# Eight chunks of the conditioning product moved from the value stage to the attention stage of a one-core encoder block

## The chip, the cores and the metric

The kernel runs on one core of a Trainium2 chip. The metric is device time in microseconds, median of three runs. The engines are named as the profile names them: PE (TensorE matmuls), PEld (its weight loads), DVE (VectorE), ACT (ScalarE), POOL (GpSimd) and SP (SyncE, whose queue issues nearly all DMAs here).

## The reference

One encoder block on x of 1024 positions by 1024 channels. Only the lines that touch the change:

```python
ada = jax.nn.silu(c) @ w_ada[i] + b_ada[i]          # (1, 6144)
shift1, scale1, gate1, shift2, scale2, gate2 = [t[:, None, :] for t in jnp.split(ada, 6, axis=-1)]
h = rmsnorm(x, g_mix[i]) * (1 + scale1) + shift1
proj = h @ w_in[i]                                   # q, k, v of two attentions, two gates
...
x = x + gate1 * (merged @ w_out[i])
h2 = rmsnorm(x, g_ffn[i]) * (1 + scale2) + shift2
...
x = x + gate2 * (glu @ w_down[i])
```

The first third of the product, shift1 and scale1 (2048 of 6144 columns), is needed at once. The other 4096 columns, gate1, shift2, scale2 and gate2, are first used after the attention: `ada[:, 24:32]` by `dshift` (L1001), `ada[:, 32:40]` by `am2` (L497), `ada[:, 16:24]` in `out_tile` (L1016), the rest in `acc` (L983) and at the end.

## The kernel before

**Planner.** All instructions are written in Python in program order. Outside blocks marked `manual_schedule` a planner orders them on each engine: at each moment of its own timeline an engine takes, of what is ready, the instruction that stands earliest in the program. A tile gets a buffer of its pool when its first writer is placed, so loads into one kind of buffer are served in program order. The order that results is fixed; on the chip each engine runs it in order.

**Product in halves.** Every projection is an fp32 product made of three fp32r matmuls: a weight tile of 128 columns is loaded as 512 KB into a `wraw` buffer (`w_load`, L58; there are two), split by ACT into `whi` (L55) and by POOL into `wlo` (L56; two of each), and `product` (L72) issues for each of eight k and each half of the positions `whi*hi`, `whi*lo`, `wlo*hi` (L77 to L79) into one of two PSUM banks `pj`. `q_half`, `k_half` and `gate_tile` empty the bank (ACT L392, L427, L732; DVE L393, L429). The `wraw` buffer is free once it is split.

**Conditioning product.** One chunk is 512 columns. `ada_load` (L126) loads its eight row tiles as four 512 KB transfers; DVE scales the first by silu(c) (L155) and adds the other seven to it (L157, 128x512 each, all in SBUF); `ada_sums` (L135) sums over partitions with four 128x1 matmuls against a column of ones (L141, in the profile eight of them, two passes each) into a PSUM tile `pada`; `ada_bias` adds the bias (L148). Chunks 0 to 3 feed norm1 in a prologue ordered by hand. Chunk 4 and 5 end that prologue (L351, L368, L369). Chunks 6 to 11 follow the value products in the loop at L485, two after each half of the value columns.

**Stages.** Prologue with norm1 (to about 100 us), the value products of both branches (L247 to L249, to about 182 us), the attention stage, the gate products that are left, then the merge, the FFN and the final norm. In the attention stage the program has for n = 0 to 7: `attend_dil` or `attend_na` of head pair n, then the q and k products of pair n+1 (`qk_tiles`), then `counts[n]` gate tiles (2, 2, 2, 2, 1, 1, 0); the last six gate tiles stand behind the loop. The q, k and gate products run while attention work waits; below they are called fillers. Attention itself uses PSUM tiles `S`, `T` and `O` (two each): scores (L557, L587, L683), a bias add and maximum on DVE (L541, L687), exponential on ACT, transposes into `T`, a split by ACT and DVE, and the product into `O`.

Of the kernel before, what the change touches and what calls it, by code (L numbers as in the profile page):

```python
# [9 lines left out]
FT = mybir.dt.float32  # L10
FR = mybir.dt.float32r
AF = mybir.ActivationFunctionType
OP = mybir.AluOpType
# [5 lines left out]
KT = 8  # L19
# [6 lines left out]
NA_NC = (6, 8, 8, 6)  # L26


def hybrid_encoder(tc, xT, c, w_ada, small, w_in, p1_bias, p23_bias, na_bias, ln2_mult, ident, w_br, w_out,
                   w_up, w_down, out):  # L30
    nc = tc.nc
    act, dve, pool, pe, sp = nc.scalar, nc.vector, nc.gpsimd, nc.tensor, nc.sync
# [83 lines left out]
    slots = iter(range(1 << 20))  # L116

    def wada_tile(j):
        n = next(slots) if j < 4 else -1
        if n == 0:  # L120
            return qkpool.tile([128, 2, 512], FT, name="kl")
        if n > 0 and (n - 1) % 6 < 2:
            return early.tile([128, 2, 512], FT, name="wada", bufs=2)
        return adapool.tile([128, 2, 512], FT, name="wada", bufs=4)

    def ada_load(j):  # L126

        rows = []
        for t in range(0, KT, 2):
            wt = wada_tile(j)  # L130
            sp.dma_start(wt, w_ada[j][:, t:t + 2])
            rows += [wt[:, i] for i in range(2)]
        return rows

    def ada_sums(parts, pa=None, stop=True, n=4):  # L135

        first = pa is None
        pa = ps_s.tile([128, 4], FT, name="pada", bufs=1) if first else pa
        for i, (w, col) in enumerate(parts):
            for m in range(n):  # L140
                pe.matmul(pa[:, m:m + 1], w[:, m * 128:(m + 1) * 128], col, start=first and i + m == 0,  # L141
                          stop=stop and i == len(parts) - 1 and m == n - 1, skip_group_check=True)
        return pa

    def ada_bias(c0, pa, n=4):

        cc = slice(c0, c0 + n)
        dve.tensor_tensor(ada[:, cc], pa[:, :n], b_ada[:, cc], OP.add)  # L148

    def ada_rows(wt, ts, acc=None):  # L150

        for t in ts:
            if acc is None:
                acc = wt[t]
                dve.tensor_scalar(acc, acc, cs[:, t:t + 1], None, OP.mult)  # L155
            else:
                dve.scalar_tensor_tensor(acc, wt[t], cs[:, t:t + 1], acc, OP.mult, OP.add)  # L157
# [6 lines left out]

    def ada_join(wt, a, b):
        dve.tensor_tensor(wt[a], wt[a], wt[b], OP.add)

    def ada_chunk(j, wt):
        ada_rows(wt, range(KT))
        ada_bias(4 * j, ada_sums([(wt[0], ones)]))  # L170

    def x_load(hf, ks=range(KT)):
        x = []
# [114 lines left out]
    with tc.manual_schedule(engines={e.engine for e in (sp, act, dve, pool, pe)}):  # L288
        x = [x_load(0)]
        sp.dma_start(sm, small)  # L290
        wt = {0: ada_load(0)}
        qk_raw = [wpool.tile([128, KT, 128], FT, name="wraw") for _ in range(2)]
        half_load(qk_raw, (0, 4), 0)
        v_raw = [qkpool.tile([128, KT, 128], FT, name="kl") for _ in range(2)]
        half_load(v_raw, (8, 9), 0)
        wt[1] = ada_load(1)
        wt[2] = ada_load(2)
        half_load(qk_raw, (0, 4), 1)
        half_load(v_raw, (8, 9), 1)
        wt[3] = ada_load(3)  # L300
        qk_w = [[wpool.tile([128, KT, 128], FR, name=n) for n in ("whi", "wlo")] for _ in range(2)]
        v_w = [v_tiles()]
        qk_psum = [ps_g.tile([128, 512], FT, name="pj") for _ in range(2)]

        accs = sq_accs()
        square(x[0], accs, range(8), dve)
        pcol = square_sums(accs)
        pb = norm_bcast(pcol)
        ada_rows_pool(wt[0], range(3))
        ada_rows(wt[0], range(3, 7))  # L310
        ada_join(wt[0], 3, 0)
        bc = to_sbuf(pb)
        pa = ada_sums([(wt[0][7], cs[:, 7:8]), (wt[0][3], ones)])
        scale_x(x[0], pb, None, range(2), dve)
        qk_split(0, (pool, dve))
        v_split(v_raw, (pool, dve), slice(0, 4), v_w[0])
        scale_x(x[0], pb, bc, range(2, 4), pool)
        piece_bias(0, pa)
        modulate(x[0], 0, range(2), (dve, dve))
        qk_products(range(2))  # L320
        pvs = [v_banks()]
        ada_rows_pool(wt[1], range(3))
        for q in range(1, 4):
            ks, c = range(2 * q - 2, 2 * q), 2 * q
            p = (0, 3, 4, 4)[q]
            ada_rows(wt[q], range(p, (8, 7)[q > 1]))
            ada_join(wt[q], p, 0)
            pa = ada_sums([(wt[q][7], cs[:, 7:8])], stop=False) if q > 1 else None
            v_products(0, (0, 1), ks)
            pa = ada_sums([(wt[q][p], ones)], pa)  # L330
            v_products(0, (2, 3), ks)
            if q == 1:
                scale_x(x[0], pb, bc, range(4, 6), pool)
            if q == 2:
                qk_split(1, (pool, dve))
                v_split(v_raw, (pool, dve), slice(4, 8), v_w[0])
                scale_x(x[0], pb, bc, range(6, 8), pool)
            if q < 3:
                ada_rows_pool(wt[q + 1], range(4))
            else:  # L340
                x.append(x_load(1, range(4)))
                v_raw1 = v_load(0, 1)
                x[1] += x_load(1, range(4, 8))
                accs = sq_accs()
                square(x[1], accs, range(3), dve)
            piece_bias(q, pa)
            modulate(x[0], 0, range(c, c + 2), (dve, dve))
            qk_products(range(c, c + 2))
        v_products(0, range(4), range(6, 8))
        v_w.append(v_split(v_raw1, (dve, pool)))  # L350
        ada_w = ada_load(4)  # L351
        square(x[1], accs, range(3, 8), dve)
        for st in range(4):
            v_out(0, 0, st, pvs[0][st])
        pvs.append(v_banks())
        v_products(1, (0,), range(8))
        pcol = square_sums(accs)
        v_products(1, (1,), range(8))
        pb = norm_bcast(pcol)
        v_products(1, (2, 3), range(8))  # L360
        bc = to_sbuf(pb)
        scale_x(x[1], pb, bc, range(0, 8, 2), dve)
        scale_x(x[1], pb, bc, range(1, 8, 2), pool)
        modulate(x[1], 1, range(4), (dve, pool))
        for st in range(4):
            v_out(0, 1, st, pvs[1][st])
        modulate(x[1], 1, range(4, 8), (dve, pool))
        ada_chunk(4, ada_w)  # L368
        ada_chunk(5, ada_load(5))  # L369

    def qk_tiles(br, pr, ws=None, ps=None):
        qt, kt = ((0, 4), (12, 16))[br]
# [112 lines left out]
    for br in range(2):  # L485
        for hv in range(2):
            w = v_split(v_load(br, hv), (pool, pool)) if br else v_w[hv]
            for st in range(8):
                if br or st > 3:
                    v_out(br, hv, st, v_product(st, w))  # L490
            if br == 0:
                va_chunks(slice(hv * 256, hv * 256 + 256))
            for j in range(2):
                jj = 6 + 4 * br + 2 * hv + j
                if jj < 12:
                    ada_chunk(jj, ada_load(jj))
    dve.scalar_tensor_tensor(am2, ada[:, 32:40], 1.0, g_ffn, OP.add, OP.mult)  # L497
    work.release()
    adapool.release()
    early.release()  # L500
# [225 lines left out]
    def gate_tile(t):  # L726
        w = weights(w_in[24 + t], pool)
        for hf, cols in enumerate(halves):
# [3 lines left out]
            act.activation(g, p, AF.Copy)  # L732
            sp.dma_start(g_scr[t][:, cols], g)

    gspool = tc.alloc_tile_pool(name="gs", bufs=2, side="right", reuse_waits="tile")
    with tc.tile_pool(name="at", bufs=2, reuse_waits="tile") as work:
        lnm = sm_pool.tile([128, 384], FT, name="lnm", bufs=1)
        sp.dma_start(lnm, ln2_mult)
        counts = (2, 2, 2, 2, 1, 1, 0, 6)
        for n in range(8):  # L740
            (attend_dil, attend_na)[n // 4](n % 4, qk, work)
            if n == 0:
                for hv in range(2):
                    vb_chunks(slice(hv * 256, hv * 256 + 256))
            if n < 7:
                qk = qk_tiles((n + 1) // 4, (n + 1) % 4)
                for t in range(sum(counts[:n]), sum(counts[:n + 1])):
                    gate_tile(t)
    for t in range(sum(counts[:7]), 16):
        gate_tile(t)  # L750
    sm_pool.release()
    ps_a.release()
    ps_l.release()
# [492 lines left out]
    with tc.manual_schedule(engines={dve.engine}):  # L1246
        for hf, cs in ((0, slice(0, 512)), (1, slice(0, 256)), (1, slice(256, 512))):
            n = cs.stop - cs.start
            late = []
# [98 lines left out]
def _layout(x, c, w_ada, b_ada, g_mix, w_in, rel_bias, na_rpb, w_branch_dil, w_branch_na, w_out, g_ffn, w_up, conv_w,  # L1348
# [6 lines left out]
    return {  # L1355
        "xT": x[0][_POS].T.reshape(KT, 128, S),
        "c": c[0].reshape(128, KT),
        "w_ada": np.concatenate([wa[:, :, :2048].reshape(128, KT, 2, 4, 256).transpose(3, 0, 1, 2, 4)
                                 .reshape(4, 128, KT, 512),
                                 wa[:, :, 2048:].reshape(128, KT, 8, 512).transpose(2, 0, 1, 3)]),  # L1360
        "small": np.concatenate([_cols(v) for v in (b_ada[0], g_mix[0], g_ffn[0], g_final, conv_w[0], conv_b[0])],
                                axis=1),
        "w_in": _rows(w_in[0]),
# [30 lines left out]
```

## Time and profile before

| what | value |
|---|---|
| three runs | 1584.0, 1585.63 and 1587.24 us; median 1585.63 |
| the profiled execution | 1584.23 us, its span 1582.5 us |
| granted TensorE clock, mean | 0.983 |
| `wada<-w_ada` transfers | 47 (and one into `kl`) of 512 KB, median 5.1 us to landing |
| HBM read, written | 158.73 MB, 42.47 MB |

The span is the time from the first to the last recorded instruction; the profiled execution's own time is 1.7 us longer. PE durations are modelled and overlap: a 128x512 matmul is shown with some 400 ns while the next one starts 230 ns later, so whether PE works back to back is read from the starts and from the idle time before a group, not from durations.

### The profile page before, as it was taken

Reading aid. Unit: us, or ns where it says so; the run is one execution under the profiler, and the core shown is the slowest. Engines: PE = TensorE matmul, PEld = TensorE weight load, DVE = VectorE, ACT = ScalarE, POOL = GpSimd, SP = SyncE. Lnnn points to the kernel's source line nnn. Section 1 sums busy time; section 2 is a strip of 40 time slices with the busy share of each in tenths; the row PEclk is TensorE's granted clock in tenths of the full one; section 3 lists DMA queues with packets and bytes.
Section 4 is the critical chain, followed back from the end, with each engine's and each line's share of the span. In section 5 each row is a group of like instructions: output and inputs, shape, how many; then the busy total and the mean of one; then the engine's idle time right before and its main releaser. Section 6 shows DMA issues by size and latency. Waiting matters only on the chain. (4 is left out here: it accounts for less than half of the span.)

```text
span 1582.5 us, 21902 instructions
## 1 busy us (share of the span) xinstructions
PE 1499.8 (95%) x7884; PEld 1280.9 (81%) x7884; DVE 1067.7 (67%) x1904; ACT 816.6 (52%) x1463; POOL 772.0 (49%) x491
## 2 busy tenths in 40 slices
PE   4898899999999999999999888999999998999998
PEld 3898888888988888888888777888888887778787
DVE  6886476666768676535424799876666667787765
ACT  4532175766666677554335454444444446475542
POOL 4452033332324444421246758676666665679621
PEclk9898999999999999999999999999999999999999
DMA  6749922232224444456634212222222224533313
GB/s 232 265 138 322 273 73 74 78 92 72 73 67 121 133 115 116 149 169 214 192 129 157 93 53 80 99 89 81 80 86 88 80 74 147 168 111 120 113 54 107
DMA packets 113269, 196.86 MB, mean 124 GB/s; under 512 B 40073, under 2 KB 61449, under 8 KB 113161
## 3 DMA queue, kind: packets, MB, share of 16 engines
q1 hardware_dynamic: 112888, 195.20, 38.2%
q8 instruction: 62, 1.02, 0.3%
q14 instruction: 47, 0.38, 0.1%
q10 hardware_dynamic: 272, 0.26, 0.1%
HBM read 158.73 MB, written 42.47 MB: 127 GB/s over the span
## 5 line engine op out<-in xcount | busy, mean ns | idle before, releaser
L56 POOL TENSOR_TENSOR wlo<-wraw,whi 128x1024 fp32r<-128x1024 f32 (+2 forms) x78 | 179.8, 2305 | 286.4 <-ACT whi L55 272.5
L77 PE MATMUL pj<-h,whi 128*128 128x512 f32 x448 | 181.4, 406 | 17.5 <-DVE kl L429 9.8
L78 PE MATMUL pj<-h,whi 128*128 128x512 f32 x448 | 179.9, 402 | 0.9 <-DVE h L215 0.9
L79 PE MATMUL pj<-h,wlo 128*128 128x512 f32 x448 | 179.8, 401 | 0.0
L56 POOL TENSOR_TENSOR wsl<-big,wsh 128x1024 fp32r<-128x1024 f32 (+1 forms) x45 | 109.1, 2427 | 50.4 <-ACT wsh L55 50.3
L1080 DVE SCALAR_TENSOR_TENSOR big<-wc,sm,big 128x256 f32<-128x256 f32 (+1 forms) x132 | 119.1, 950 | 17.3 <-ACT big L1074 17.2
L55 ACT ACTIVATE whi<-wraw 128x1024 fp32r<-128x1024 f32 (+2 forms) x81 | 81.1, 1001 | 78.5 <-PE pj L78 45.4
L77 PEld LDWEIGHTS pj<-h,whi 128*128 128x128 f32 x448 | 85.4, 191 | 35.4 <-issue 7.0
L78 PEld LDWEIGHTS pj<-h,whi 128*128 128x128 f32 x448 | 85.6, 191 | 16.7 <-DVE h L215 2.2
L79 PEld LDWEIGHTS pj<-h,wlo 128*128 128x128 f32 x448 | 85.6, 191 | 15.4
L542 ACT ACTIVATE P<-P,st 128x256 f32<-128x256 f32 x128 | 64.2, 503 | 47.5 <-DVE st L541 47.1
L541 DVE CUSTOM_DVE_ANT_0 P<-S,bias 128x256 f32<-128x256 f32 x128 | 52.2, 421 | 47.9 <-PE S L588 36.2
L474 POOL TENSOR_TENSOR vv<-vv 96x256 fp32r<-96x256 f32 (+2 forms) x32 | 40.9, 1288 | 83.5 <-ACT vv L473 64.1
L157 DVE SCALAR_TENSOR_TENSOR wada<-wada,cs 128x512 f32<-128x512 f32 x67 | 66.5, 993 | 18.5 <-DMA wada<-w_ada 16.5
L1080 DVE SCALAR_TENSOR_TENSOR big<-pj,sm,big 128x512 f32<-128x512 f32 x132 | 67.9, 565 | 16.1 <-ACT big L1074 16.1
L694 POOL TENSOR_SCALAR P<-P,stb 128x288 f32<-128x288 f32 (+1 forms) x32 | 40.1, 1253 | 78.3 <-DVE stb L691 59.5
L429 DVE SCALAR_TENSOR_TENSOR kl<-pj,ks 64x512 fp32r<-64x512 f32 x64 | 56.3, 880 | 30.8 <-ACT ks L427 30.2
L1074 ACT ACTIVATE big<-wc,sm 128x512 f32<-128x512 f32 x44 | 35.8, 815 | 76.5 <-DVE wc L897 46.1
L247 PE MATMUL pv<-vwh,h 128*128 128x256 f32 x256 | 74.2, 290 | 0.0
L249 PE MATMUL pv<-vwh,h 128*128 128x256 f32 x256 | 73.7, 288 | 0.0
L248 PE MATMUL pv<-vwl,h 128*128 128x256 f32 x256 | 73.1, 287 | 0.0
L56 POOL TENSOR_TENSOR wsl<-wraw,wsh 128x768 fp32r<-128x768 f32 (+1 forms) x23 | 49.8, 2166 | 43.3 <-ACT wsh L55 43.3
(363 smaller groups left out, 4888.6 us busy)
## 6 DMA issues: line engine op xcount, KB each, us to landing
wada<-w_ada SPq DMA_DIRECT2D x47, 512.0 KB, 5.1
wraw<-w_in SPq DMA_DIRECT2D x36, 512.0 KB, 3.8
big<-w_up SPq DMA_DIRECT2D x22, 512.0 KB, 5.4
wraw<-w_up SPq DMA_DIRECT2D x22, 512.0 KB, 3.7
as<-big SPq DMA_DIRECT2D x22, 512.0 KB, 3.0
big<-as SPq DMA_DIRECT2D x22, 512.0 KB, 7.4
wraw<-w_down SPq DMA_DIRECT2D x24, 384.0 KB, 3.8
gs<-gs SPq DMA_DIRECT2D x32, 256.0 KB, 2.0
```

The lines of the kernel that those rows point to most:

```text
L55: act.activation(hi, raw, AF.Copy)
L56: lo_eng.tensor_tensor(lo, raw, f(hi), OP.subtract)
L77: pe.matmul(psum, whi[:, k0 + k], mhi, start=k == 0, stop=False)
L78: pe.matmul(psum, whi[:, k0 + k], mlo, start=False, stop=False)
L79: pe.matmul(psum, wlo[:, k0 + k], mhi, start=False, stop=k == n - 1)
L157: dve.scalar_tensor_tensor(acc, wt[t], cs[:, t:t + 1], acc, OP.mult, OP.add)
L247: pe.matmul(p, hhi, hi[:, k], start=fresh and k == 0, stop=False, skip_group_check=True)
L248: pe.matmul(p, hhi, lo[:, k], start=False, stop=False, skip_group_check=True)
L249: pe.matmul(p, hlo, hi[:, k], start=False, stop=k == KT - 1, skip_group_check=True)
L429: dve.scalar_tensor_tensor(ll[x], pp[a], 0.125, f(kh[a]), OP.mult, OP.subtract)
L542: act.activation(pp, pp, AF.Exp, bias=mi, scale=-1.0, accum_out=li)
L1080: dve.scalar_tensor_tensor(y[:, dst], src, wt, y[:, dst], OP.mult, OP.add)
```

## The change

Chunks 4 to 11 leave the prologue and the value loop. Their 4096 columns are laid out anew as 32 tiles of 128 columns (`w_ada2`), each loaded by the same `w_load` into a `wraw` buffer: 8 k-rows of 128 columns, 512 KB, one transfer. DVE does the same scale and seven adds, now on 128x128; one 128x1 product (two passes) goes into a PSUM tile of the tag `T`; a 128x1 bias add ends it. In the loop two such tiles stand behind each `qk_tiles` and one behind each gate tile; one ahead of each of the last six gate tiles; the two that are left and `am2` behind those. Per block the `wraw` requests thus read q, k, a, a, g, a, g, a, where a is a conditioning tile.

```diff
     def wada_tile(j):
-        n = next(slots) if j < 4 else -1
+        n = next(slots)
...
-    def ada_sums(parts, pa=None, stop=True, n=4):
+    def ada_sums(parts, pa=None, stop=True, n=4, new=None):
         first = pa is None
-        pa = ps_s.tile([128, 4], FT, name="pada", bufs=1) if first else pa
+        if first:
+            pa = new if new is not None else ps_s.tile([128, 4], FT, name="pada", bufs=1)
...
-    def ada_chunk(j, wt):
-        ada_rows(wt, range(KT))
-        ada_bias(4 * j, ada_sums([(wt[0], ones)]))
...
-        ada_w = ada_load(4)
...
-        ada_chunk(4, ada_w)
-        ada_chunk(5, ada_load(5))
...
-            for j in range(2):
-                jj = 6 + 4 * br + 2 * hv + j
-                if jj < 12:
-                    ada_chunk(jj, ada_load(jj))
-    dve.scalar_tensor_tensor(am2, ada[:, 32:40], 1.0, g_ffn, OP.add, OP.mult)
...
+    late = iter(range(16, 48))
+
+    def late_ada(n):
+
+        for j in itertools.islice(late, n):
+            w = w_load(w_ada2[j - 16])
+            ada_rows([w[:, t] for t in range(KT)], range(KT))
+            ada_bias(j, ada_sums([(w[:, 0], ones)], n=1, new=ps_a.tile([128, 512], FT, name="T")), 1)
+
...
                 qk = qk_tiles((n + 1) // 4, (n + 1) % 4)
+                late_ada(2)
                 for t in range(sum(counts[:n]), sum(counts[:n + 1])):
                     gate_tile(t)
+                    late_ada(1)
     for t in range(sum(counts[:7]), 16):
+        late_ada(1)
         gate_tile(t)
+    late_ada(32)
+    dve.scalar_tensor_tensor(am2, ada[:, 32:40], 1.0, g_ffn, OP.add, OP.mult)
```

On the host the second part of `w_ada` becomes `wa[:, :, 2048:].reshape(128, KT, 32, 128).transpose(2, 0, 1, 3)`.

More of the change, by code (lines that the diff above doesn't have):

```diff
@@ L26, with hybrid_encoder @@
 NA_NC = (6, 8, 8, 6)
-def hybrid_encoder(tc, xT, c, w_ada, small, w_in, p1_bias, p23_bias, na_bias, ln2_mult, ident, w_br, w_out,
+def hybrid_encoder(tc, xT, c, w_ada, w_ada2, small, w_in, p1_bias, p23_bias, na_bias, ln2_mult, ident, w_br, w_out,
                    w_up, w_down, out):
@@ L118, in wada_tile @@
     def wada_tile(j):
-        n = next(slots) if j < 4 else -1
+        n = next(slots)
         if n == 0:
             return qkpool.tile([128, 2, 512], FT, name="kl")
-        if n > 0 and (n - 1) % 6 < 2:
+        if (n - 1) % 6 < 2:
             return early.tile([128, 2, 512], FT, name="wada", bufs=2)
@@ L1357, in _layout @@
         "c": c[0].reshape(128, KT),
-        "w_ada": np.concatenate([wa[:, :, :2048].reshape(128, KT, 2, 4, 256).transpose(3, 0, 1, 2, 4)
-                                 .reshape(4, 128, KT, 512),
-                                 wa[:, :, 2048:].reshape(128, KT, 8, 512).transpose(2, 0, 1, 3)]),
+        "w_ada": wa[:, :, :2048].reshape(128, KT, 2, 4, 256).transpose(3, 0, 1, 2, 4).reshape(4, 128, KT, 512),
+        "w_ada2": wa[:, :, 2048:].reshape(128, KT, 32, 128).transpose(2, 0, 1, 3),
         "small": np.concatenate([_cols(v) for v in (b_ada[0], g_mix[0], g_ffn[0], g_final, conv_w[0], conv_b[0])],
```

## The prediction

> **What bounds the kernel now.** I read the page's busy line first, then sums by stage, then the PE's order of time where a stage shows idle PE, then the raw buffers' instructions and the fillers' evacuations.
>
> ```profile
> PE 1499.8 (95%) x7884; PEld 1280.9 (81%) x7884; DVE 1067.7 (67%) x1904; ACT 816.6 (52%) x1463; POOL 772.0 (49%) x491
> ...
> L157 DVE SCALAR_TENSOR_TENSOR wada<-wada,cs 128x512 f32<-128x512 f32 x67 | 66.5, 993 | 18.5 <-DMA wada<-w_ada 16.5
> ```
>
> PE is the busy engine, so only what PE waits for can be won; the second row is the chunks' adds. By stage (columns: stretch, its length, busy time of PE, PEld, DVE, ACT, POOL, granted clock, DMA share, GB/s):
>
> ```profile
> 95.00:200.00 105.00, 93.36 (x697) 89.84 (x696) 66.31 (x89) 23.99 (x45) 23.69 (x14) 0.94 0.83 267
> 200.00:660.00 460.00, 445.88 (x2752) 393.94 (x2752) 312.64 (x849) 312.87 (x711) 169.59 (x123) 1.00 0.32 95
> 660.00:720.00 60.00, 60.00 (x316) 51.09 (x315) 23.79 (x44) 32.28 (x59) 15.90 (x8) 1.00 0.56 184
> ```
>
> The value stage, which the chunks leave, has 11.6 us of idle PE, a clock of 0.94 and a DMA share of 0.83. The attention stage, which takes them, has PE at 97%, DVE at 68% and the DMA at a third. PE's order of time in the value stage:
>
> ```profile
> 130.61 1.84 PE L141 MATMUL pada<-ones,wada 128*128 128x1 f32 x8 [6.77 <-issue]
> ```
>
> ```profile
> 191.78 0.95 PE L141 MATMUL pada<-ones,wada 128*128 128x1 f32 x8
> ...
> 193.15 0.40 PE L79 MATMUL pj<-h,wlo 128*128 128x512 f32 x1
> 198.34 0.58 PE L557 MATMUL S<-ks,qs 128*128 128x256 f32 x1 [4.79 <-DVE st L541]
> ```
>
> The 11.6 us are two waits. At 130.61 PE stands before a chunk's sum, in order, while value products behind it could run; the sum waits for DVE, and DVE for w_ada (the 16.5 us of the L157 row). At 198.34 it waits for attention's first scores to be taken up. Each idle time is followed by half the clock:
>
> ```profile
> 130.00:135.00 5.00, 4.39 (x20) 4.42 (x21) 4.93 (x6) 0.82 (x2) 2.55 (x1) 0.50 0.70 205
> 135.00:140.00 5.00, 5.00 (x39) 5.00 (x38) 3.24 (x5) 0.89 (x3) 0.00 (x0) 0.87 0.87 320
> ...
> 200.00:205.00 5.00, 4.98 (x25) 4.69 (x25) 3.28 (x14) 4.98 (x15) 2.53 (x2) 0.54 0.40 122
> ```
>
> **The change, part by part.** *The wait and its clock go.* 6.77 us idle; from 130.61 to 135 half of 4.39 us (2.2) and from 135 to 140 0.13 of 5 (0.65): 9.6 us. Other loads keep the DMA busy there, but in this stage PE waits for none of them.
>
> *The entry to attention.* What is late there is a POOL chain:
>
> ```profile
> 194.53 2.34 POOL L56 TENSOR_TENSOR wlo<-wraw,whi 128x1024 fp32r<-128x1024 f32 x1 [44.36 <-ACT whi L55]
> 196.83 0.99 POOL L531 TENSOR_TENSOR bias<-bias,lnm 128x384 f32<-128x384 f32 x1
> ```
>
> The first attention bias is queued on POOL behind the lower half of a gate's weights, which waited 44 us for a `whi` buffer that the fillers free. The buffers of chunks 10 and 11 no longer hold up attention's SBUF, but whether the planner writes this POOL order again I can't see. It is worth 0 to 4.79 + 0.46 x 5 (2.3) = 7.1 us; I take half, 3.5. Front gain: 13.1 us (9.6 to 16.7).
>
> *PE work.* Eight groups of eight sums (0.95 us each, 7.6 us) leave a stage that PE then fills, and 64 sums of the same shape return to one that it also fills: zero, no cover needed. SP issues 32 transfers of 512 KB as before (eight chunks of four).
>
> *DVE work.* The trace has no 128x128 add of this form. The bounds:
>
> ```profile
> L148 DVE TENSOR_TENSOR ada<-pada,sm x8: 149/161/165, 104.3 to 192.8; 128x4 f32<-128x4 f32 x8
> ```
>
> ```profile
> L1256 DVE SCALAR_TENSOR_TENSOR x<-pj,ada,x x24: 454/479/751, 1527.1 to 1573.3; 128x256 f32<-128x256 f32 x16, 128x512 f32<-128x512 f32 x8
> ```
>
> Between 161 ns at 4 columns and 454 at 256, half way is 305 ns; eight such and a bias add are 2.6 us a tile (1.45 to 3.8). Of the 32 tiles, 14 + 10 = 24 lie in the loop: 62 us (35 to 91) on DVE's 312.6 of 460, 81% (76 to 88). DVE does not become the bound; attention's work covers the adds. [...] If DVE is late next, PE waits at the fillers' bank:
>
> ```profile
> PE pj L77 <- DVE kl L429: 9.8, 8, 2.0
> ```
>
> This is all of PE's waiting for the evacuation of k from 420 to 660 us (from 200 to 420 the same view has none). With DVE a fifth busier I add a fifth: 2 us (0 to the port case below).
>
> *The raw buffers.* This decides. In attention:
>
> ```profile
> L55 ACT ACTIVATE whi<-wraw x25: 1041/1045/1064, 224.0 to 659.5; 128x1024 fp32r<-128x1024 f32 x25
> L56 POOL TENSOR_TENSOR wlo<-wraw,whi x24: 2377/2396/2410, 225.1 to 646.7; 128x1024 fp32r<-128x1024 f32 x24
> ...
> DMA to landing us min/median/max: 3.6/3.7/4.3
> ```
>
> ```profile
> 244.18 0.33 SPq L60 DMA_DIRECT2D wraw<-w_in  x1
> 260.76 0.33 SPq L60 DMA_DIRECT2D wraw<-w_in  x1
> ```
>
> ```profile
> 276.74 1.08 ACT L392 ACTIVATE qs<-pj 64x512 fp32r<-64x512 f32 x2
> 286.77 1.19 ACT L427 ACTIVATE ks<-pj 64x512 fp32r<-64x512 f32 x2
> ...
> 299.09 1.20 ACT L427 ACTIVATE ks<-pj 64x512 fp32r<-64x512 f32 x2
> 302.75 0.60 ACT L732 ACTIVATE gs<-pj 128x512 f32<-128x512 f32 x1 [0.37 <-PE pj L79]
> ```
>
> A weight tile is loaded some 40 us ahead of its evacuation: k's, loaded at 244.18, is evacuated from 286.77; the gate's, at 260.76, from 302.75. The fillers come in program order without a gap: q, k, gate. Now two conditioning tiles stand between k and the gate. They get both `wraw` buffers as soon as q's and k's weights are split, which is when the one before ends. DVE has their sums within microseconds, but the buffer is free only after the 128x1 product on PE, and that stands behind q and k in the program: while filler matmuls of q and k are ready, PE takes those. So both buffers stay taken until the last matmul of k, and the gate's weights are requested only then: load 3.7, ACT 1.05, POOL 2.4, the sums ahead of them 0.5: a hole of 7.6 us without a filler, once behind each of seven k. SP's queue stands at that request in order, with attention's bias and v loads behind it. In a hole PE has attention alone:
>
> ```profile
> 200.00:660.00 460.00, 321.80 (x1396) 231.30 (x1397) 68.53 (x82) 77.50 (x105) 1.00 0.32 95
> ```
>
> These are the instructions on `pj` alone: fillers take 321.8 of 460, so attention has 30% of PE, or 44% if it speeds up to where DVE and ACT (both 313 of 460) are full. I take the latter, 56% idle: 4.3 us a hole (5.3 at 70%). From 420 on the fillers have gaps of their own, where a sum can slip in; of the seven, four come before (k of pairs 1 to 4) and count in full, three by half: 5.5 x 4.3 = 24 us, between 0 if sums always slip in and 7 x 5.3 = 37. The eight tiles outside the loop alternate one to one with gates, DVE is at 40% there, and I cost them at nothing; uncovered, they are 8 x 2.6 us of DVE.
>
> *Sum* against the profiled execution, 1584.23 us: -13.1 + 2 + 24 = +12.9, 1597.1. The median of the runs is 1.4 above that execution: **1598 us**.
>
> **The rivals.** *The sums slip in* (faster). If attention work leaves PE moments without a ready filler in the planner's timeline, the sums go early and no hole opens. For it: the gaps of 9.8 us from 420 on. Against it: none before 420, and in the value stage, where value products stand ahead of the next pair's q whose weights were split by then, no instruction touches `pj` for 48 us:
>
> ```profile
> 132.00:180.00 48.00, 0.00 (x0) 0.00 (x0) 0.00 (x0) 0.00 (x0) 0.96 0.96 323
> ```
>
> 1584.23 - 13.1 + 2 + 1.4 = 1574.5. It decides on whichever side more than about three of the seven holes are missing (13.1 - 2 over 4.3 = 2.6 holes pay the gain back).
>
> *A draw.* Only the wait at 130.61 is won (9.6), the POOL order stays, and two holes open (8.6): 1584.23 - 9.6 + 2 + 8.6 + 1.4 = 1586.6.
>
> *The port* (slower still). Minimum, median and maximum of the chunks' adds in ns, then one of them beside a split on POOL:
>
> ```profile
> L157 DVE SCALAR_TENSOR_TENSOR wada<-wada,cs x67: 745/752/2852, 16.0 to 186.6; 128x512 f32<-128x512 f32 x67
> ```
>
> ```profile
> 126.98 2.75 DVE L157 SCALAR_TENSOR_TENSOR wada<-wada,cs 128x512 f32<-128x512 f32 x1 [1.40 <-DMA wada<-w_ada]
> ```
>
> ```profile
> 126.83 2.34 POOL L56 TENSOR_TENSOR vwl<-wraw,vwh 128x1024 fp32r<-128x1024 f32 x1 [10.56 <-ACT vwh L55]
> ```
>
> A DVE add on SBUF that starts inside a POOL split ends after it: 2.75 us instead of the median 0.75. In attention POOL is busy 37%, 123 operations in 460 us, so a tile of 2.6 us meets about one (0.37 + 0.7); at half a split, 1.2 us, that is 29 us on DVE. DVE is in order, so softmax and evacuations stand behind it. If PE had no slack for it: -9.6 + 37 + 29 + 1584.23 + 1.4 = 1642. It decides if PE's waits for DVE grow several times over 9.8 us. [...]
>
> **How the numbers follow.** The forecast 0.49, sums slip in 0.36, draw 0.09, port 0.06. A measurement of this kernel can tell some 0.2% (3.2 us) from no change, so faster 0.36, same 0.09, slower 0.55. The forecast's own range goes from 1589 (half the holes) to 1614 (seven at 5.3 with the lesser front gain: 1584.23 - 9.6 + 37 + 2 = 1613.6). The range for 8 in 10 reaches down to the first rival with the whole front gain (1584.23 - 16.7 + 1.4 = 1569): 1569 to 1614. Above it lies the port, beside it the tails.
>
> **What would show it.** Front: no wait of several microseconds ahead of a 128x1 sum in the value stage, clock 1.00 there, and the value products ending some 16 us earlier (9.6 and the sums that left). Holes: behind each k's last evacuation a stretch of about 8 us in which PE has no L77, `wraw` requests of gates no longer 40 us ahead but right behind two sums, and SP waits of L60 that end on PE instead of POOL. Slip: sums amid the matmuls of q and k, and requests as early as before. Port: the new 128x128 adds with a mean well over their minimum, and PE waits ending on DVE L541 or L429. The forecast is wrong if attention plus gates are not longer than before by some 26 us (24 and 2), or if they are and PE waits elsewhere.

## The result, and the profile after

The changed kernel takes **1713.74 us** (median of four runs, 1710.02 to 1717.73), the kernel before 1584.88 beside it: a ratio of 1.081, 95% interval 1.0786 to 1.0833. It is slower, as forecast, but by 129 us and not by 13. The profiled execution has a span of 1710.5 us.

The page of the changed kernel, its head, then the groups of the new scales and adds (columns as in the prediction's rows):

```profile
span 1710.5 us, 22090 instructions
...
PE 1572.9 (92%) x7884; PEld 1332.4 (78%) x7884; DVE 1096.5 (64%) x2120; ACT 822.3 (48%) x1463; POOL 771.5 (45%) x491
...
L156 DVE TENSOR_SCALAR wraw<-wraw,cs 128x128 f32<-128x128 f32 x32 | 22.7, 708 | 116.8 <-DMA wraw<-w_ada 116.4
...
L158 DVE SCALAR_TENSOR_TENSOR wraw<-wraw,cs 128x128 f32<-128x128 f32 x224 | 83.3, 375 | 5.3
```

By stage:

```profile
95.00:200.00 105.00, 95.60 (x695) 91.65 (x694) 20.23 (x55) 32.78 (x72) 24.75 (x15) 0.93 0.44 128
200.00:660.00 460.00, 408.72 (x2232) 352.85 (x2231) 302.52 (x869) 251.65 (x565) 128.31 (x94) 0.88 0.29 91
660.00:840.00 180.00, 162.13 (x814) 136.18 (x813) 105.09 (x269) 80.48 (x165) 49.25 (x34) 0.90 0.44 140
```

The front is no faster worth speaking of (idle PE 9.4 us instead of 11.6, and the clock 0.93 beside 0.94). The attention stage has lost: in the same 460 us PE issues 2232 matmuls instead of 2752, ACT 565 operations instead of 711, and the clock is 0.88. The last gate's evacuation ends at 838.9 us instead of 717.2: 122 of the 128 us between the two spans are lost by then.

What is missing are the fillers. PE on `pj` alone (the projections) from 195 to 660 us, in the kernel before and in the changed one:

```profile
195.00:660.00 465.00, 321.80 (x1396) 0.99 0.33 96
```

```profile
195.00:660.00 465.00, 250.37 (x1103) 0.88 0.29 91
```

71 us of filler work is pushed out behind the attention, where gates then run with nothing to lie beside. This number is the gauge of the experiments below. In several stretches of the changed kernel there is no filler at all; two of them (first all work, then `pj` alone):

```profile
214.00:245.00 31.00, 22.14 (x132) 19.77 (x133) 27.03 (x98) 22.37 (x58) 6.68 (x6) 0.84 0.20 50
313.00:338.00 25.00, 17.05 (x98) 14.83 (x99) 23.27 (x79) 17.75 (x45) 6.66 (x6) 0.78 0.19 47
```

```profile
214.00:245.00 31.00, 0.00 (x0) 0.84 0.20 50
313.00:338.00 25.00, 0.00 (x0) 0.78 0.19 47
```

DVE is 87 and 93% busy here, so attention alone runs close to DVE's pace. What ends the first hole is seen in the order of time on PE and on SP's queue:

```profile
213.36 1.21 ACT L421 ACTIVATE ks<-pj 64x512 fp32r<-64x512 f32 x2
```

```profile
243.43 1.08 PE L641 MATMUL T<-idt,P 128*128 128x128 f32 x4 [0.64 <-DVE u L643]
...
245.17 0.84 PE L142 MATMUL T<-ones,wraw 128*128 128x1 f32 x4
```

```profile
245.62 0.35 SPq L60 DMA_DIRECT2D wraw<-w_in  x1
246.06 0.38 SPq L60 DMA_DIRECT2D wraw<-w_ada  x1
247.85 0.33 SPq L648 DMA_DIRECT2D oa<-u  x1
252.92 0.33 SPq L60 DMA_DIRECT2D wraw<-w_in  x1
```

ACT evacuates the last of k at 213. The adds of the two tiles that hold the raw buffers were over long before, in DVE's order of time:

```profile
148.70 3.21 DVE L158 SCALAR_TENSOR_TENSOR wraw<-wraw,cs 128x128 f32<-128x128 f32 x10
```

But their sums run at 245.17, right behind the last transposes of the running attention (L641), 93 us after the adds; 0.45 us later the gate's weights are requested, and that attention's output is stored at 247.85. The sum waits not for k but for the end of the attention whose `T` buffers stand ahead of it. The waits of SP's queue and of DVE say the same (line waited for: total us, times, longest):

```profile
SPq L60 <- PE T L142: 105.9, 23, 16.3
```

```profile
DVE ada L149 <- PE T L142: 65.1, 12, 11.0
```

### The profile page after: what moved, and what is told of

Same layout as the page of the kernel before. It is cut to its first block, busy times and chain, and to the rows that moved or that the text cites. A ratio compares the mean times of both kernels' runs of the same rounds, so it can differ in the third digit from the quotient of the medians.

```text
span 1710.5 us, 22090 instructions
## 1 busy us (share of the span) xinstructions
PE 1572.9 (92%) x7884; PEld 1332.4 (78%) x7884; DVE 1096.5 (64%) x2120; ACT 822.3 (48%) x1463; POOL 771.5 (45%) x491
## 4 chain that ended last, share of the span: by engine, by line
PE 48%; DVE 8%; POOL 4%; DMA 3%; issue 2%; ACT 2%; SPq 0%; DVEq 0%; POOLq 0%; ACTq 0%
PE pj L888 9%; PE pj L887 9%; PE pj L889 9%; PE pj L77 6%; PE pj L79 6%; PE pj L78 6%; DVE big L1083 2%; PE O L705 1%; PE pj L396 1%; POOL wlo L56 1%; POOL wsl L56 1%; DMA wraw<-w_ada 1%; ACT ks L421 1%; PE S L672 1%; DVE kl L423 1%
## 5 line engine op out<-in xcount | busy, mean ns | idle before, releaser
L77 PE MATMUL pj<-h,whi 128*128 128x512 f32 x448 | 185.6, 415 | 12.1 <-ACT h L209 6.4
L78 PE MATMUL pj<-h,whi 128*128 128x512 f32 x448 | 183.9, 410 | 2.1 <-DVE h L212 2.1
L77 PEld LDWEIGHTS pj<-h,whi 128*128 128x128 f32 x448 | 88.5, 198 | 29.8 <-ACT whi L55 6.7
L78 PEld LDWEIGHTS pj<-h,whi 128*128 128x128 f32 x448 | 88.8, 198 | 20.6 <-DVE h L212 3.2
L156 DVE TENSOR_SCALAR wraw<-wraw,cs 128x128 f32<-128x128 f32 x32 | 22.7, 708 | 116.8 <-DMA wraw<-w_ada 116.4
L158 DVE SCALAR_TENSOR_TENSOR wraw<-wraw,cs 128x128 f32<-128x128 f32 x224 | 83.3, 375 | 5.3
```

What stands on the lines that cost most here:

```text
L77: pe.matmul(psum, whi[:, k0 + k], mhi, start=k == 0, stop=False)
L78: pe.matmul(psum, whi[:, k0 + k], mlo, start=False, stop=False)
```

## The experiments

Nearly all are edits of the changed kernel; "none" is 1581.5 us, the run without late tiles (`e4_none`). The body they touch is this (`late_ada`):

```python
w = w_load(w_ada2[j - 16])
ada_rows([w[:, t] for t in range(KT)], range(KT))
ada_bias(j, ada_sums([(w[:, 0], ones)], n=1, new=ps_a.tile([128, 512], FT, name="T")), 1)
```

### First round: bank, hold, priority, nothing

**The sum in the fillers' bank.**

```diff
-ada_bias(j, ada_sums([(w[:, 0], ones)], n=1, new=ps_a.tile([128, 512], FT, name="T")), 1)
+ada_bias(j, ada_sums([(w[:, 0], ones)], n=1, new=ps_g.tile([128, 512], FT, name="pj")), 1)
```

> The 32 sums go into a bank of the fillers (pj) instead of T; raw buffers, order and all else as in the changed kernel. In the changed kernel no filler runs from 214 to 245 us and in three like stretches, and the held sums run as attention's transposes end. Theory BANK (the sums wait for a T bank, which attention's own transposes take first, and hold both raw buffers meanwhile): the four long holes shrink to some 8 us, about 4 x 27 us less, 1590 to 1625. Rival ORDER (the sums wait on PE behind whatever stands ahead of them in the program, in any bank): no change, 1700 to 1720. Rival DVE (the loss is DVE standing in order at w_ada transfers, 116 us in all): no change either, 1690 to 1715.

One run: 1658.59 us. In between: 55 us better, more than 70 still lost. The sums now come right behind k, as I had forecast for the change itself (in brackets the wait before it, and what ended it: here DVE, which empties the fillers' bank):

```profile
295.50 0.38 PE L142 MATMUL pj<-ones,wraw 128*128 128x1 f32 x2 [0.34 <-DVE kl L423]
```

**The last add into a buffer of its own**, so that DVE alone frees the raw buffer; P gives one of five buffers for the space.

```diff
+acc = latepool.tile([128, 128], FT, name="late")
-ada_rows([w[:, t] for t in range(KT)], range(KT))
+ada_rows([w[:, t] for t in range(KT - 1)], range(KT - 1))
+dve.scalar_tensor_tensor(acc, w[:, KT - 1], cs[:, KT - 1:KT], w[:, 0], OP.mult, OP.add)
...
```

> The last of the eight adds writes to a small buffer of its own (128x128, six of them; the attention's P buffers go from five to four to make room), so a raw buffer is free after the adds, not after the sum; the sums stay in T. BANK and ORDER both say that it is the held raw buffers which starve the fillers: no hole, 1570 to 1600. DVE: the adds and their waits are all still there, 1680 or more.

One run: 1657.5 us, in between again.

**Late tiles left out.**

```diff
-w = w_load(w_ada2[j - 16])
-ada_rows([w[:, t] for t in range(KT)], range(KT))
-ada_bias(j, ada_sums([(w[:, 0], ones)], n=1, new=ps_a.tile([128, 512], FT, name="T")), 1)
+dve.tensor_copy(ada[:, j:j + 1], b_ada[:, j:j + 1])
```

> Leaves out the 32 late tiles altogether: no load, no adds, no sum (the 32 columns hold the bias alone). It shows what the first half of the change wins by itself. By the forecast's steps: 9.6 to 16.7 us of waits and clock and 7.6 us of sums less than before, 1561 to 1569. If the value stage has new waits of its own (in the changed kernel PE waits 9.4 us there for ACT to empty value banks), less than 5 us of gain beside the sums: 1572 to 1578.

1581.54 us, ratio 0.9965 (0.9949 to 0.9981). A miss on my side: the whole front is worth some 5 us, not 13, with the 7.6 us of sums gone too. So the late tiles cost 132 us.

**The sum at high priority.**

```diff
+with tc.high_priority():
+    pa = ada_sums([(w[:, 0], ones)], n=1, new=ps_a.tile([128, 512], FT, name="T"))
+ada_bias(j, pa, 1)
```

> The sums alone are given a high priority for the planner, so each takes the next free T bank and the next free moment of PE, ahead of attention and of fillers; raw buffers are then held for little more than the adds. BANK and ORDER: no holes, 1570 to 1595. DVE: 1680 or more, since loads and adds keep their order.

1716.24 us, ratio 1.0817 (1.079 to 1.0844): the time doesn't change. The edit did take hold: the first sums run at 242.35 us instead of 245.17, the next at 257.58 instead of 266.34. But they still come only at the end of the attention block. So it is not that the planner prefers other matmuls that are ready; the sum isn't ready, as one that waits for its buffer would not be.

### Second round: parts alone

**Bank and buffer together**: the two edits of `e1_pj` and `e2_acc`.

> The own accumulator of the last add (which frees the raw buffer on DVE instead of on PE) and the fillers' PSUM bank for the sum, both at once. Each alone took about 56 us off the changed kernel (1658.6 and 1657.5 against 1713.7). If they remove two different waits the gains add up: 1595 to 1615. If both remove the same wait (the raw buffers held by a late sum), the gain comes only once and the rest is DVE standing at the transfers and adding: 1645 to 1660.

1671.07 us, ratio 1.0538 (1.0507 to 1.0569): no better than either alone. The gains don't add up.

**The loads alone.**

```diff
 w = w_load(w_ada2[j - 16])
+dve.tensor_scalar(ada[:, j:j + 1], w[:, 0, 0:1], cs[:, 0:1], None, OP.mult)
```

> All late transfers stay, into the raw buffers, but of each tile DVE does one operation on 128x1 and nothing else: seven adds, the scale, the sum on PE and the bias are left out, so the output isn't the reference's. STAND (DVE waits in its order for each transfer, with softmax and evacuations behind it): most of the loss stays, 1640 or more, with DVE waits at w_ada of 75 us or more. HELD (the raw buffers wait for a sum that stands late on PE): gone, 1580 to 1605. ADDS (the DVE time of the adds and their contention with POOL): gone, 1580 to 1605. The extra wait for a buffer per filler alone, without any hold, should cost at most one load a tile that is hidden.

1583.97 us, ratio 0.9979 (0.9964 to 0.9994). STAND falls: 32 transfers of 512 KB through the raw buffers, and DVE waiting for them in order, cost 2.4 us over none, and the two intervals overlap. The fillers keep their pace:

```profile
195.00:660.00 465.00, 319.63 (x1396) 0.99 0.41 123
```

**Adds and sums on resident data, no loads**, with the own buffer and four P.

```diff
-w = w_load(w_ada2[j - 16])
+dve.tensor_scalar(acc, f(h[0, 0][0][:, 0:128]), cs[:, 0:1], None, OP.mult)
+for t in range(1, KT):
+    dve.scalar_tensor_tensor(acc, f(h[0, t][0][:, 0:128]), cs[:, t:t + 1], acc, OP.mult, OP.add)
...
```

> The late adds (one scale, seven multiply-adds of 128x128 for each of the 32 tiles, into a small buffer of their own) read a resident tile of normed activations instead of a load; sums and bias stay in T. The late loads are left out, so the output isn't the reference's; P has four buffers instead of five. ADDS: DVE's added 60 us in the loop and its contention cost as much as before, 1640 or more. STAND and HELD: neither a transfer nor a raw buffer is waited for, 1580 to 1600. In between would mean that adds and waits share the loss.

1645.97 us, ratio 1.0378 (1.0347 to 1.0409).

**The control for P**, an edit of the kernel before, at four places.

```diff
-P = sm_pool.tile([128, 2, 256], FT, name="P", bufs=5)
+P = sm_pool.tile([128, 2, 256], FT, name="P", bufs=4)
```

> The kernel before with four P buffers instead of five: the control for the runs with an accumulator of their own, which gave one P buffer away. If the buffer is slack: 1581 to 1592. If softmax needs it, 1620 or more, and part of what those runs still lost is this.

1605.69 us, ratio 1.013 (1.0097 to 1.0164). The buffer isn't slack: 18 us. The runs with an own buffer (`e2_acc`, `e6_both`, `e8_resident`) therefore carry some 18 us that are not the change's, and `e8_resident` lies about 47 us over none (1646.0 - 17.8 - 1581.5) rather than 64, if the 18 us simply add.

### Third round: hold without adds, adds without hold

**Load, hold, scale and sum in T; no adds.**

```diff
-ada_rows([w[:, t] for t in range(KT)], range(KT))
+dve.tensor_scalar(w[:, 0], w[:, 0], cs[:, 0:1], None, OP.mult)
```

> The late tiles keep their load, their raw buffer, one scale on DVE and the sum in T on PE with its bias; the seven adds of each tile are left out, so the output isn't the reference's. HOLD (raw buffers and the T bank stand behind a sum that comes late on PE, whatever DVE does): some 60 us over the run without late tiles (1581.5), 1630 to 1650. If the hold costs something only because the adds delay the sums: 1582 to 1600.

1710.5 us, ratio 1.0783 (1.0742 to 1.0825): with one short DVE operation a tile instead of eight, the whole loss is there. The changed kernel's 224 adds cost 3 us on top of the hold, which the spread of the runs does not tell from nothing, and the filler gauge is the changed kernel's own:

```profile
195.00:660.00 465.00, 250.83 (x1107) 0.90 0.30 93
```

**The adds alone**, into one scratch buffer, five P, and **half of them** (`range(1, KT // 2)`).

```diff
+late_acc = sm_pool.tile([128, 128], FT, name="late", bufs=1)
-w = w_load(w_ada2[j - 16])
-ada_rows([w[:, t] for t in range(KT)], range(KT))
-ada_bias(j, ada_sums([(w[:, 0], ones)], n=1, new=ps_a.tile([128, 512], FT, name="T")), 1)
+dve.tensor_scalar(late_acc, f(h[0, 0][0][:, 0:128]), cs[:, 0:1], None, OP.mult)
+for t in range(1, KT):
+    dve.scalar_tensor_tensor(late_acc, f(h[0, t][0][:, 0:128]), cs[:, t:t + 1], late_acc, OP.mult, OP.add)
+dve.tensor_copy(ada[:, j:j + 1], b_ada[:, j:j + 1])
```

> The adds alone: eight 128x128 operations a tile on resident activations into one scratch buffer that nothing reads; no late load, no sum on PE, P with its five buffers; the output isn't the reference's. Over the run without late tiles (1581.5). ADDS (DVE stands on the path of attention, so its added time of about 2.7 us x 24 tiles in the loop and the port waits are paid): 1625 to 1650. If what the resident run lost was the sums, the T bank or the smaller P: 1582 to 1600.

> As the run with the adds alone, with four of the eight operations a tile; the output isn't the reference's. If every added DVE microsecond is paid: half the loss of that run. If DVE has slack for the first part and overflows beyond it: under a quarter of the loss. If it is a cost per group (where the group stands in DVE's order), more than two thirds of it.

1613.23 us, ratio 1.0174 (1.0131 to 1.0217), and 1595.4, ratio 1.0056 (1.0035 to 1.0077): 32 and 14 us over none, about in proportion. All work to 363 us in the run with the full adds, then in the run with none (columns of the stage view):

```profile
195.00:363.00 168.00, 149.54 (x779) 125.13 (x778) 159.63 (x455) 90.29 (x215) 46.51 (x33) 0.91 0.20 62
```

```profile
195.00:363.00 168.00, 164.66 (x959) 143.05 (x958) 114.34 (x329) 112.17 (x270) 59.63 (x43) 1.00 0.26 77
```

As nothing waits for these adds, the planner put them all ahead of 363 us, where DVE is then 95% busy and PE issues 180 matmuls fewer. So this run shows that DVE has too little slack for them, at another density than in the change.

**A candidate: late work only behind the loop**, as 512-column pieces of two rows (64 adds of 128x512), through the raw buffers.

```diff
-w = w_load(w_ada2[j - 16])
+w = w_load(w_ada2[j // 4][:, 2 * (j % 4):2 * (j % 4) + 2].rearrange("p t (a n) -> p (t a) n", a=4))
+w = w.rearrange("p (t a) n -> p t (a n)", t=2)
...
+    lates[0] = latepool.tile([128, 512], FT, name="late")
...
+dve.scalar_tensor_tensor(acc, w[:, 1], cs[:, t:t + 1], acc, OP.mult, OP.add)
...
-                late_ada(2)
-                    late_ada(1)
...
         gate_tile(t)
+        late_ada(6)
```

> A candidate: no late work beside attention. The eight chunks are loaded as 512-column pieces of two rows into the raw buffers only between the six gates behind the loop and after them, 64 operations of 128x512 on DVE in place of 256 of 128x128, into an accumulator of their own, so that DVE alone frees the raw buffer; 32 sums on PE. If the tail's DVE (40% busy) and its raw buffers hide it: 1578 to 1588, level with the kernel before or up to 5 us better. If the gates wait for raw buffers, or the pieces run on into the merge and hold up its weights: 1595 to 1640.

1664.23 us, ratio 1.0501 (1.0453 to 1.0549). Between the gates PE is now half idle, where it had no idle time before (stage view below). SP requests four pieces from 682.23 us and the next gate's weights only at 692.72, behind them. From 655 to 850 us PE waits 22.3 us for the split of the gates' weights and 15.2 us, in its order, at the pieces' sums.

```profile
660.00:700.00 40.00, 19.30 (x94) 16.29 (x92) 24.08 (x47) 14.28 (x29) 4.25 (x3) 0.61 0.49 154
```

### Fourth round: bank and hold apart

**The bank without the hold.**

```diff
-ada_rows([w[:, t] for t in range(KT)], range(KT))
-ada_bias(j, ada_sums([(w[:, 0], ones)], n=1, new=ps_a.tile([128, 512], FT, name="T")), 1)
+dve.tensor_scalar(ada[:, j:j + 1], w[:, 0, 0:1], cs[:, 0:1], None, OP.mult)
+ada_bias(j, ada_sums([(f(h[0, 0][0]), ones)], n=1, new=ps_a.tile([128, 512], FT, name="T")), 1)
```

> The bank without the hold: late loads with one short DVE operation that frees the raw buffer, and a sum in T over a resident tile, with its bias; adds are left out and the sum's operand is another, so the output isn't the reference's. Without late sums 1584.0, with hold and bank 1710.5. BANK ALONE (DVE's bias stands in order for a sum that stands behind the attention's transposes in T): 1640 or more. HOLD: 1585 to 1600, as no filler waits for this sum.

1592.71 us, ratio 1.0033 (1.0019 to 1.0047). The late sum in `T`, with DVE's bias standing for it, costs 9 us when it holds no buffer of the fillers.

**The hold without the bank**, an edit of `e9_hold`.

```diff
-ada_bias(j, ada_sums([(w[:, 0], ones)], n=1, new=ps_a.tile([128, 512], FT, name="T")), 1)
+ada_bias(j, ada_sums([(w[:, 0], ones)], n=1, new=ps_g.tile([128, 512], FT, name="pj")), 1)
```

> The hold without the bank: load, raw buffer, one scale and the sum as in the run without adds, but the sum in the fillers' bank pj; seven adds a tile are left out, so the output isn't the reference's. BOTH TOGETHER (the hold hurts because the sum stands behind T): 1600 to 1630, holes of some 8 us behind each k, as I had forecast. RAW ALONE: 1640 or more, with fillers still missing for 20 us a block.

1632.88 us, ratio 1.0279 (1.0251 to 1.0306), 3 us over the bound I gave. The four corners, without adds: loads alone 1584.0, bank 1592.7 (+8.7), hold 1632.9 (+48.9), both 1710.5 (+126.5). The two together cost 69 us more than their sum: the hold lasts as long as the sum is late, and `T` makes it late. The corner "hold" is not a pure one: its sums take turns in the fillers' bank instead, and how much of the 49 us that costs was not tried. The gauge (`pj` alone to 660 us) of the bank, then of the hold:

```profile
195.00:660.00 465.00, 319.08 (x1380) 0.98 0.39 119
```

```profile
195.00:660.00 465.00, 298.69 (x1351) 0.97 0.37 112
```

**The late tiles ahead of the attention in the program**, all else as changed.

```diff
+            if n < 7:
+                late_ada(2 + counts[n])
             (attend_dil, attend_na)[n // 4](n % 4, qk, work)
...
-                late_ada(2)
-                    late_ada(1)
```

> Hold, bank and adds all as in the changed kernel, but in the loop the late tiles stand in the program ahead of the attention block instead of behind its q and k, so that their T buffers go round before that block's transposes; the numbers come out the same. ORDER OF T (the sum waits because its turn in T comes after the running attention): most of the loss goes, what stays is the adds' 32 us and some: 1610 to 1645. If the place in the program doesn't matter: 1690 or more.

1667.88 us, ratio 1.0518 (1.0489 to 1.0546): 46 us better from the place in the program alone, less than expected. Part of the shortfall is a new loss at the entry to attention: from 182 to 205 us PE is busy 14.87 us, and 23.00 in the changed kernel. The holes are shorter but not gone; one of the stretches without a filler, on `pj` alone:

```profile
262.00:279.00 17.00, 0.13 (x1) 0.73 0.52 170
```

In this stretch two sums run at 262.88 and 263.84 us, again right behind a block's last transposes (L641, 262.44). Only then are two more tiles loaded into the raw buffers (263.70), and the next weights of q, k or a gate are requested at 273.07, when these have been added and summed as well. So the place in the program sets how late the sum is. That it does so by the turn in `T` fits `e1_pj` and `e5_prio`, but this edit moves the tiles' turn in the raw buffers too.

**The candidate with two buffers of its own** in the space that attention leaves, behind all gates.

```diff
-w = w_load(w_ada2[j // 4][:, 2 * (j % 4):2 * (j % 4) + 2].rearrange("p t (a n) -> p (t a) n", a=4))
-w = w.rearrange("p (t a) n -> p t (a n)", t=2)
+w = latepool.tile([128, 2, 512], FT, name="lraw")
+sp.dma_start(w, w_ada2[j // 4][:, 2 * (j % 4):2 * (j % 4) + 2])
...
```

> A candidate: as the run with 512-column pieces behind the loop, but the pieces have two buffers of their own in the space that attention leaves, and stand in the program behind all gates. If the loss of that run (1664.2) was the gates' raw buffers: 1578 to 1600. If it is the place of the pieces ahead of the merge (its operands wait for their space, DVE for their transfers): 1620 or more.

1676.87 us, ratio 1.0561 (1.0538 to 1.0583). The gates are on time (the last evacuation ends at 716.6), but then the pieces run alone to 803 us. The merge's first products come only at 803.1, though ACT and DVE have split their operands by 728.5: PE stands in its order at the eight sums, which run ahead of them. The stage view, then PE's wait (from 640 to 1000 us):

```profile
750.00:800.00 50.00, 8.50 (x38) 8.19 (x37) 28.23 (x46) 0.00 (x0) 0.00 (x0) 0.50 0.62 199
```

```profile
PE T L142 <- DVE late L741: 73.3, 8, 12.8
```

### Fifth round: the tail alone

```diff
+    def late_none(n):
+        for j in itertools.islice(late, n):
+            dve.tensor_copy(ada[:, j:j + 1], b_ada[:, j:j + 1])
...
-                late_ada(2)
+                late_none(2)
-                    late_ada(1)
+                    late_none(1)
```

> Of the 32 late tiles only the eight behind the loop stay as they are in the changed kernel; of the 24 in the loop nothing is loaded, added or summed, so the output isn't the reference's. Without any late tile 1581.5. TAIL AT NOTHING: 1578 to 1588. TAIL OF ITS OWN (each gate's raw buffer is free only when the sum of the tile before it has run, so load, adds and sum of a tile stand in the chain of the last gates): 4 to 11 us a tile for the six between gates, 1600 to 1640.

1618.39 us, ratio 1.0182 (1.0146 to 1.0218): 37 us over none, for eight tiles that I had put at nothing. The same wait, at the last attention block: no filler for 35 us (`pj` alone), until the sums follow that block's last transposes and the gate's weights are requested.

```profile
648.00:683.00 35.00, 0.20 (x1) 0.80 0.54 170
```

```profile
676.87 1.05 PE L693 MATMUL T<-idt,P 128*128 128x128 f32 x4
678.27 0.58 PE L142 MATMUL T<-ones,wraw 128*128 128x1 f32 x2
```

```profile
678.88 0.33 SPq L60 DMA_DIRECT2D wraw<-w_in  x1
```

## Why the prediction was wrong

**The raw buffers: the right mechanism, with the wrong thing waited for.** This is the step that failed. I had named this term as the one that decides, and what holds was as I said: the tiles take both raw buffers, DVE is done with them early, the sum on PE comes late, and SP stands at the gate's request. But I wrote that the sum "stands behind q and k in the program", so that the buffers are free at k's end and a hole is one load and split, 7.6 us. I had looked at PE's order alone and not at the sum's own output: a `T` buffer, which it gets only after the transposes of the attention block written ahead of it. The hole then lasts until that block's end, 31 and 25 us in the two stretches shown. The runs show it from four sides: sum in `pj`, sums right behind k and 55 us back (`e1_pj`); without adds, 1710.5 with `T` and 1632.9 with `pj`; the same tiles earlier in the program, 46 us back (`e14_first`); higher priority, nothing (`e5_prio`). The term of 24 us (0 to 37) was some 95 in the loop: 132 in all less the 37 of the tail alone, if these add.

**The tail at nothing: wrong, 37 us.** I had asked whether DVE covers the adds and not asked of the tail what I had asked of the loop, whose buffer a tile holds and until when.

**The front: -13.1 forecast, about -5 measured** (none: 0.9965; the loads alone: 0.9979). The wait of 6.77 us ahead of the chunk's sum did go, but another came in its place. In the changed kernel ACT stands in order at the next weights' transfer, with the evacuations of the value banks behind it, and PE waits for a bank:

```profile
131.21 0.72 SPq L451 DMA_DIRECT2D vab<-vas  x1
131.97 0.64 SPq L453 DMA_DIRECT2D vab<-vas  x1
132.66 0.46 SPq L252 DMA_DIRECT2D vbc<-vs  x1
133.23 0.37 SPq L60 DMA_DIRECT2D wraw<-w_in  x1
```

```profile
138.13 1.06 ACT L55 ACTIVATE whi<-wraw 128x1024 fp32r<-128x1024 f32 x1 [10.10 <-DMA wraw<-w_in]
```

```profile
PE pv L244 <- ACT vs L251: 9.4, 2, 5.7
```

The weights were requested at 133.23, behind the value copies in SP's queue. I had written that PE waits for none of the other loads in this stage; that was true of the order before, and the new one made such a wait. The stage's end moved by 2.8 us (181.6 to 178.8), not 16. The entry to attention did lose its wait: from 182 to 205 us PE is now busy throughout at full clock.

```profile
182.00:205.00 23.00, 23.00 (x134) 19.89 (x133) 12.13 (x32) 12.39 (x32) 0.00 (x0) 1.00 0.17 44
```

**DVE's adds: size about right, price near by luck.** By line (minimum, median and maximum in ns, from 195 to 850 us):

```profile
L158 DVE SCALAR_TENSOR_TENSOR wraw<-wraw,cs x210: 329/352/2539, 253.2 to 834.4; 128x128 f32<-128x128 f32 x105
L156 DVE TENSOR_SCALAR wraw<-wraw,cs x30: 271/289/2372, 250.7 to 831.7; 128x128 f32<-128x128 f32 x30
```

The 128x128 add took 352 ns and the scale 289 (medians), where I had estimated 305 for each: 2.75 us a tile against 2.44, without the bias add. By their means (708 for the scale, 375 for the adds) it is 3.3. I priced the adds at +2, and in the changed kernel they cost about 3. That is luck: with shorter holes the same adds cost 26 (`e1_pj`, one run of 1658.6, against `e13_raw`, 1632.9), and without the raw buffers' hold some 32 (`e10_adds`) to 47 (`e8_resident`, with its sums). That the long holes hide them fits these numbers but was not tried by itself. So "attention's work covers the adds" was wrong as well.

**The port rival: its parts are there, its bound not reached.** One scale that started inside a POOL split ended with it (252.98 and 252.89 us) and took 2.27 us instead of the median 0.29 (DVE, then POOL):

```profile
250.71 2.27 DVE L156 TENSOR_SCALAR wraw<-wraw,cs 128x128 f32<-128x128 f32 x1 [1.78 <-DMA wraw<-w_ada]
```

```profile
250.53 2.36 POOL L56 TENSOR_TENSOR wlo<-wraw,whi 128x1024 fp32r<-128x1024 f32 x1 [0.39 <-ACT whi L55]
```

By the means over the medians this is at most 19 us on DVE for all 32 tiles (32 x 0.42 + 224 x 0.023), where I had said 29 for the loop; no run shows what PE pays for it, and none that a port is the cause.

**The signs I had named.** Requests of gates right behind two sums, and SP's raw-buffer waits ending on PE: seen as written. Holes of about 8 us: 31 and 25. Clock 1.00 in the value stage: 0.93. Sums slipping in amid q and k: in no dilated block. Attention plus gates longer by some 26 us: longer by 124 (from 178.8 to 838.9 us, where it had been from 181.6 to 717.2). One sum does not come out: half the holes with the other terms kept give 1586.5 (1598.5 - 12), not the 1589 of the range's lower end.

**What stays open.** How the 49 us of the hold alone divide between loop and tail: `e13_raw` ends its gates at 756.3 instead of 717.2, so 39 of them arise by there, but `e15_tail` has bank and adds in it and can't be subtracted. In `e6_both` some 72 us over none are left (1671.1 - 17.8 - 1581.5), more than the adds alone cost: there SP's raw-buffer requests wait 58.5 us for DVE's last add, so a hold remains and ends on DVE; its share was not tried. No version that computes the whole product beats the kernel before: with this order of the front the most that the move can win is the 4 to 5 us of `e4_none` and `e7_loads`, and both candidates lost (75 and 90).

## What to carry to other kernels

Before work is put into buffers of another stream, ask of each of its instructions which buffer it writes and whose turn comes before it: sums of half a microsecond kept two 512 KB buffers from the fillers for some 30 us, because their PSUM tiles stood behind a whole attention block. An operand's buffer was free when its last reader had run (the gate's weights were requested 0.45 us after the sums that held the buffers had begun), so the reader with the worst place in the order sets the price, and two waits in one chain can cost more than their sum (here +9 and +49 alone, +127 together). Ask the same of every place where the work was put: the one I costed at nothing was worth 37 us.

## What was not expected of the hardware

A 128-column multiply-add on SBUF took DVE 352 ns and a 512-column one 752 ns (medians). On a straight line through the two, that is an estimated fixed part of about 219 ns (352 - 128 x 400/384): cutting a chunk into 128-column tiles takes 4 x 352 = 1408 ns for 752 of work. And the clock was lower in the holes: 0.84, 0.78, 0.67 and 0.50 were granted in the stretches without fillers (from 214, 313, 404 and 506 us), where the kernel before had 1.00 in all four. That it falls from hole to hole is not a rule: in the run without adds (`e9_hold`) the same four windows had 0.87, 0.89, 0.85 and 0.73. The last two of the changed kernel:

```profile
404.00:429.00 25.00, 18.75 (x98) 16.99 (x99) 23.26 (x79) 17.86 (x45) 6.67 (x6) 0.67 0.19 46
506.00:521.00 15.00, 10.24 (x44) 9.35 (x44) 13.04 (x42) 9.10 (x20) 2.44 (x3) 0.50 0.26 63
```
